# Twelve weight loads moved from GpSimd's queue to SyncE's queue, each in two halves

## The chip, the core and the metric

The kernel runs on one core of one Trainium2 chip. The time is device microseconds of one execution of the whole program; a figure for a kernel is the median of several executions. The profile is one more execution, taken by the hardware profiler. Its rows name the engines PE (TensorE matmul), PEld (TensorE weight load), DVE (VectorE), ACT (ScalarE), POOL (GpSimd) and SP (SyncE). SP computes nothing here: it only issues DMA transfers, in the order of its program. POOL issues DMA transfers too, from a queue of its own.

## The reference

One layer of a decoder trunk on 512 tokens of width 1024, all in float32:

```
h   = RMSNorm(x)
q_a,k_a,v_a, q_b,k_b,v_b, gates = split(h @ W_in)
y_a = block-sparse causal attention with rotary q, k
y_b = stick-breaking causal attention
x   = x + (sigmoid(gate_a)*(y_a @ W_a) + sigmoid(gate_b)*(y_b @ W_b)) @ W_out
h   = RMSNorm(x)
u   = causal_depthwise_conv(h @ W_up, width 3)       # W_up: 1024 x 5632
x   = x + (silu(u_gate) * u_val) @ W_down            # W_down: 2816 x 1024
out = RMSNorm(x)
```

The part that matters here is `h @ W_up`, the up-projection. Its 5632 columns are handled as 22 pairs of column tiles of 128, a gate tile and a value tile in each pair.

## The kernel before

**Three products for one.** A float32 product is made of three TensorE passes: both operands are split into a high part (`hi`, a rounded copy, made by ACT) and a low part (`lo`, what the rounding left, made by DVE), and `mm3` adds hi*hi (line 75), hi*lo (line 76) and lo*hi (line 77). In the up-projection the first operand of each pass is the weight, so line 77 is the pass that reads the low part of the weight, `wlo`; lines 75 and 76 read `whi`.

**Seven products for eight.** Tile pairs 4 to 15 (`MIXED`) use a Strassen-like scheme: seven quarter products (256 columns of tokens each, 12 matmuls each) in place of eight. Their weights are four tiles, called a, b, c and d below with the pair's number behind:

- a: the raw gate tile, and b: a mix of tiles, both loaded by `first_four`;
- c: another mix of tiles, and d: half a raw value tile, both loaded by `last_three`.

a, b and c feed 24 matmuls each, d feeds 12. The mixes were summed in DRAM earlier, as `usum`. For the c tiles the low part was also made earlier, in the attention's merge (`split_ahead`), and written to DRAM as `ulo`. So for c only the high part is made on the spot, and `wlo` is loaded from `ulo` (512 KB); for a, b and d, DVE makes `wlo` (line 900).

**Order of the tiles.** TensorE's order is written out by hand: a4 b4, a5 b5, c4 d4, a6 b6, c5 d5, and so on in rounds of b, c and d of one pair after the a of another, to a15 b15, c14 d14, c15 d15. The last round differs: c15 comes right behind d14, with no a and b between. After d15 come the plain pairs 16 to 21, whose tiles are loaded by `wload` (line 65). The order of all other engines, SP and POOL among them, is set by a scheduler from the code.

**Buffers.** `wmix` takes three tiles per weight: `raw` from a pool of five, `whi` and `wlo` from pools of three. A tile's `wlo` is thus the buffer that the weight three places earlier used. For c of pair i that is d of pair i-1 (for c15 it is b15, for c4 it is b4), so the load of `ulo` into it can start only when TensorE has done the last matmul of that weight. Between the two, TensorE works on a and b of another pair, 48 matmuls; for c15 it works on c14 and d14, 36 matmuls. Of a c tile, half h=1 (columns 512 to 1023) is used first, by the first `quarter` call of `last_three`, and half h=0 by the second, 12 matmuls later.

**Queues.** All loads of `raw` are issued by SP (lines 895 and 65), five buffers ahead. The loads of `ulo` into `wlo` are issued by POOL (line 897), which has nothing else to do in this stage.

Of the kernel before, what the change touches and what calls it, by code (L numbers as in the profile page):

```python
# [10 lines left out]
F32 = mybir.dt.float32  # L11
# [30 lines left out]
def trunk_layer(ctx: ExitStack, tc: tile.TileContext, x: bass.AP, xT: bass.AP, w: bass.AP, vec: bass.AP,  # L42
                gfin: bass.AP, trig: bass.AP, out: bass.AP):
    nc = tc.nc
# [845 lines left out]
    def wmix(i, parts, n=1024, lo=None):  # L890
        raw = wraw.tile([128, 1024], F32, name="raw")
        hi = wsp.tile([128, 1024], F32R, name="whi")
        wlo = wsp.tile([128, 1024], F32R, name="wlo")
        for sl, src in parts:
            nc.sync.dma_start(raw[:, sl] if isinstance(sl, slice) else raw.rearrange("p (h c) -> p h c", h=2), src)
        if lo is not None:
            nc.gpsimd.dma_start(wlo.rearrange("p (h c) -> p h c", h=2), lo)
        nc.scalar.activation(hi[:, :n], raw[:, :n], AF.Copy)  # L898
        if lo is None:
            nc.vector.tensor_sub(wlo[:, :n], raw[:, :n], hi[:, :n].bitcast(F32))  # L900
        return hi, wlo

    def first_four(i):
        wa = wmix(i, [(slice(0, 1024), w[WIDX["up", i, 0]])])
        wb = wmix(i, [(None, both(usum[i][0:2]))])
        ps1, ps2 = up_ps(), up_ps()
        X, Q, Y, Z = ps1[:, :256], ps1[:, 256:], ps2[:, :256], ps2[:, 256:]
        quarter(X, wa, 0, rows_of(0, 0), True)
        quarter(Q, wa, 1, rows_of(1, 0), False)
        quarter(Y, wb, 1, mixed_rows(1), True)  # L910
        quarter(Z, wb, 0, mixed_rows(3), False)
        p1s, p5s, v = (tmp[i % 2][:, n] for n in range(3))
        nc.scalar.activation(p1s, X, AF.Copy)
        nc.scalar.activation(p5s, Y, AF.Copy)
        nc.vector.tensor_add(v, Z, p5s)
        return ps1, ps2, p1s, v

    def last_three(i, ps1, ps2, p1s, v):
        X, Q, Y, Z = ps1[:, :256], ps1[:, 256:], ps2[:, :256], ps2[:, 256:]
        wc = wmix(i, [(None, both(usum[i][2:4]))], lo=ulo.get(i))  # L920
        wd = wmix(i, [(slice(0, 512), w[WIDX["up", i, 1]][:, 512:])], 512)
        quarter(X, wc, 1, mixed_rows(2), False)
        quarter(Y, wc, 0, rows_of(1, 1), False)
        quarter(Z, wd, 0, mixed_rows(4), False)
        u2 = tmp[2][:, i % 2]
        nc.scalar.activation(u2, X, AF.Copy)
        u = up.tile([128, 2, S], F32, name="u", bufs=1)
        nc.vector.tensor_add(u[:, 0, :256], Q, p1s)
        nc.vector.tensor_add(u[:, 1, 256:], X, v)
        nc.vector.tensor_add(u.rearrange("p b s -> p (b s)")[:, 256:768].rearrange("p (n c) -> p n c", n=2),  # L930
                             ps2.rearrange("p (n c) -> p n c", n=2), u2[:, None].to_broadcast([128, 2, 256]))
        glu(i, (u[:, 0], u[:, 1]))
# [228 lines left out]
```

## Time and profile before

| | |
|---|---|
| median of 3 runs | 723.58 us |
| the three runs | 718.51, 723.58, 724.37 us |
| profiled execution, its own time | 722.6 us |
| its span, first to last instruction | 720.6 us |
| PE busy in the span | 705.9 us (98%) |
| DVE, ACT, POOL busy | 568.7, 392.5, 81.8 us |
| mean granted TensorE clock | 0.999 |
| stage of pairs 4 to 15 | about 416.9 to 543.4 us of the span |

The stage limits are the starts of the first and the end of the last matmul on a weight of pairs 4 to 15. In a row of the timeline the columns are the start, the duration (both us), the engine, the line, the operation, and output<-inputs; brackets give the idle time of the engine before the instruction and what ended it. A matmul's duration there includes its way through the array, so that matmuls overlap: the step from one start to the next is the time that TensorE needs for one.

### The profile page before, as it was taken

What the parts mean: (1) busy time and instruction counts of PE and PEld (TensorE: products, weight loads), DVE (VectorE), ACT (ScalarE), POOL (GpSimd) and SP (SyncE); (2) the same over time, 40 slices, a digit from 0 to 9 for tenths busy, and PEclk for the clock granted to TensorE, in tenths of its full rate; (3) what the DMA queues carried; (4) which work ended last, traced back from release to release, by engine and by line L of the source; (5) the groups of instructions that cost most, each with busy time, mean ns of one, the idle gap of its engine ahead of it and who ended that gap; (6) DMA issues with size and microseconds to landing.
All of it is one profiled execution on the core that took longest, in us unless ns stands there. A gap on an engine that the chain in (4) does not pass through costs nothing.

```text
span 720.6 us, 11212 instructions
## 1 busy us (share of the span) xinstructions
PE 705.9 (98%) x4316; PEld 611.2 (85%) x4316; DVE 568.7 (79%) x862; ACT 392.5 (54%) x585; POOL 81.8 (11%) x131
## 2 busy tenths in 40 slices
PE   9999999999999999999999999999989999999996
PEld 6888888879878888888899899999988888888884
DVE  7778867595994685749685998898898778878997
ACT  6335535463654444427485667667665445456764
POOL 1211222354002122000004100000000000000000
PEclk9999999999999999999999999999999999999999
DMA  8799999999325786537668657766773323567703
GB/s 314 273 345 366 355 234 242 239 240 254 98 88 187 257 265 230 199 114 257 227 219 239 157 167 249 239 202 227 245 251 111 109 88 93 178 196 228 272 27 118
DMA packets 45974, 151.32 MB, mean 210 GB/s; under 512 B 5216, under 2 KB 5984, under 8 KB 41824
## 3 DMA queue, kind: packets, MB, share of 16 engines
q1 hardware_dynamic: 33536, 93.64, 38.0%
q0 software_dynamic: 12096, 56.63, 28.5%
q8 instruction: 34, 0.56, 0.3%
q10 hardware_dynamic: 288, 0.33, 0.1%
q14 instruction: 20, 0.16, 0.1%
HBM read 135.90 MB, written 44.04 MB: 250 GB/s over the span
## 4 chain that ended last, share of the span: by engine, by line
PE 88%; DVE 5%; DMA 3%; issue 3%; ACT 2%; POOLq 0%; DVEq 0%; ACTq 0%
PE b L77 11%; PE b L76 11%; PE b L75 11%; PE mm L75 10%; PE mm L77 9%; PE mm L76 9%; PE c L75 4%; PE c L77 4%; PE c L76 4%; PE q L194 3%; DMA wlo<-ulo 3%; PE tp L468 3%; PE tp L446 2%; DVE R L417 1%; PE sc L370 1%
## 5 line engine op out<-in xcount | busy, mean ns | idle before, releaser
L76 PE MATMUL b<-h,whi 128*128 128x256 f32 (+1 forms) x336 | 109.1, 325 | 0.0
L75 PE MATMUL b<-h,whi 128*128 128x256 f32 (+1 forms) x336 | 108.9, 324 | 0.0
L77 PE MATMUL b<-h,wlo 128*128 128x256 f32 (+1 forms) x336 | 108.8, 324 | 0.0
L70 ACT ACTIVATE whi<-raw 128x1024 fp32r<-128x1024 f32 (+2 forms) x70 | 68.6, 986 | 72.9 <-PE b L76 28.3
L71 DVE TENSOR_TENSOR wlo<-raw,whi 128x1024 fp32r<-128x1024 f32 (+2 forms) x70 | 78.5, 1129 | 24.4 <-ACT whi L70 24.1
L75 PE MATMUL mm<-xg,whi 128*128 128x512 f32 x224 | 89.9, 402 | 0.0
L77 PE MATMUL mm<-xg,wlo 128*128 128x512 f32 x224 | 87.5, 391 | 0.0
L76 PE MATMUL mm<-xg,whi 128*128 128x512 f32 x224 | 87.5, 390 | 0.0
L76 PEld LDWEIGHTS b<-h,whi 128*128 128x128 f32 x336 | 64.0, 191 | 5.1 <-DVE h L750 0.2
L77 PEld LDWEIGHTS b<-h,wlo 128*128 128x128 f32 x336 | 64.0, 191 | 5.0
L75 PEld LDWEIGHTS b<-h,whi 128*128 128x128 f32 x336 | 64.0, 191 | 5.0
L620 ACT ACTIVATE whi<-raw 128x1024 fp32r<-128x1024 f32 x45 | 47.0, 1052 | 35.6 <-DVE raw L638 16.1
L898 ACT ACTIVATE whi<-raw 128x1024 fp32r<-128x1024 f32 (+1 forms) x48 | 45.6, 951 | 35.0 <-PE b L76 29.4
L620 DVE TENSOR_TENSOR wlo<-raw,whi 128x1024 fp32r<-128x1024 f32 x45 | 54.6, 1222 | 7.2 <-ACT whi L620 7.2
L77 PE MATMUL b<-xa,wlo 128*128 128x256 f32 x192 | 54.7, 285 | 4.7 <-DMA wlo<-ulo 4.7
L75 PE MATMUL b<-xa,whi 128*128 128x256 f32 x192 | 54.4, 283 | 0.0
L76 PE MATMUL b<-xa,whi 128*128 128x256 f32 x192 | 54.4, 283 | 0.0
L75 PEld LDWEIGHTS mm<-xg,whi 128*128 128x128 f32 x224 | 42.1, 188 | 9.8 <-issue 1.8
L77 PEld LDWEIGHTS mm<-xg,wlo 128*128 128x128 f32 x224 | 42.1, 188 | 9.1
L76 PEld LDWEIGHTS mm<-xg,whi 128*128 128x128 f32 x224 | 42.2, 188 | 7.8
L900 DVE TENSOR_TENSOR wlo<-raw,whi 128x1024 fp32r<-128x1024 f32 (+1 forms) x36 | 37.6, 1045 | 11.1 <-ACT whi L898 10.7
L77 PEld LDWEIGHTS b<-xa,wlo 128*128 128x128 f32 x192 | 36.9, 192 | 5.3 <-DMA wlo<-ulo 5.3
(267 smaller groups left out, 1649.1 us busy)
## 6 DMA issues: line engine op xcount, KB each, us to landing
raw<-w SPq DMA_DIRECT2D x113, 512.0 KB, 4.4
usum<-w POOLq DMA_DIRECT2D x12, 1024.0 KB, 26.2
raw<-usum SPq DMA_DIRECT2D x24, 512.0 KB, 4.5
usum<-w POOLq DMA_DIRECT2D x12, 512.0 KB, 20.7
usum<-usum POOLq DMA_DIRECT2D x24, 256.0 KB, 11.8
praw<-usum POOLq DMA_DIRECT2D x12, 512.0 KB, 4.9
ulo<-praw POOLq DMA_DIRECT2D x12, 512.0 KB, 3.3
wlo<-ulo POOLq DMA_DIRECT2D x12, 512.0 KB, 4.0
```

Source lines behind the costliest of these rows:

```text
L70: nc.scalar.activation(hi[:, sl], raw[:, sl], AF.Copy)
L71: nc.vector.tensor_sub(lo[:, sl], raw[:, sl], hi[:, sl].bitcast(F32))
L75: nc.tensor.matmul(ps, a[0], b[0], start=start, stop=False, **kw)
L76: nc.tensor.matmul(ps, a[0], b[1], start=False, stop=False, **kw)
L77: nc.tensor.matmul(ps, a[1], b[0], start=False, stop=stop, **kw)
L194: nc.tensor.matmul(qk0[c], w0[i][:, (k % 2) * 512 + c * 128:(k % 2) * 512 + (c + 1) * 128], xg[k][:, j], start=(k == 0 and n == 0), stop=( ...
L370: nc.tensor.matmul(scs[h // 2][:, h % 2, o:o + n], Q[i][r0:r0 + 32, c, qt * 128:(qt + 1) * 128], K[i][r0:r0 + 32, d, :n], start=False, sto ...
L446: nc.tensor.transpose(tp[:, h, c:c + 128], a[:, h, c:c + 128], ident)
L468: nc.tensor.matmul(av[h * 64:(h + 1) * 64, j, qt * 128:(qt + 1) * 128], v[:, kb, (2 * p + h) * 64:(2 * p + h + 1) * 64], aT[p][:, h, o + k ...
L620: splits.append((nc.scalar.activation(hi, raw, AF.Copy), nc.vector.tensor_sub(lo, raw, hi.bitcast(F32))))
L898: nc.scalar.activation(hi[:, :n], raw[:, :n], AF.Copy)
L900: nc.vector.tensor_sub(wlo[:, :n], raw[:, :n], hi[:, :n].bitcast(F32))
```

## The change

The load of a c tile's low part is no longer one transfer of 512 KB issued by POOL. It is two transfers of 256 KB issued by SP, half h=1 first. The bits moved are the same; the views as float32 on both sides only make the two types equal.

```
         if lo is not None:
-            nc.gpsimd.dma_start(wlo.rearrange("p (h c) -> p h c", h=2), lo)
+            for h in (1, 0):
+                nc.sync.dma_start(wlo[:, h * 512:(h + 1) * 512].bitcast(F32), lo[:, h].bitcast(F32))
         nc.scalar.activation(hi[:, :n], raw[:, :n], AF.Copy)
```

The order of instructions on PE, DVE and ACT is the same as before. POOL loses its last twelve transfers; SP gains 24. On SP, in the middle of the stage, these rows stand one behind the other in the changed program (+ marks what is new; usum_417, usum_418 and usum_419 are the mixes of pairs 10, 11 and 12, ulo_2583 and ulo_2584 the low parts of c9 and c10, `w 128x512` is a d tile, `w 128x1024` an a tile):

```order
+L898 DMA wlo<-ulo_2583 128x512 x2
 L895 DMA raw<-usum_417 128x2x512
 L895 DMA raw<-w 128x512
 L895 DMA raw<-w 128x1024
+L898 DMA wlo<-ulo_2584 128x512 x2
 L895 DMA raw<-usum_419 128x2x512
 L895 DMA raw<-usum_418 128x2x512
```

The two halves of c10 now stand ahead of the raw loads of b12 and c11 in SP's queue, and the first of them waits there for TensorE to finish d9. In most other rounds the halves stand one place later, behind the raw load of the b tile.

At the end of the stage SP's queue reads as follows (usum_422 is the mix of pair 15, here c15; ulo_2588 and ulo_2589 are the low parts of c14 and c15; the line-65 rows are the tiles of pairs 16 to 21):

```order
 L895 DMA raw<-usum_422 128x2x512
+L898 DMA wlo<-ulo_2588 128x512 x2
 L895 DMA raw<-w 128x512
-L65 DMA raw<-w 128x1024 x12
+L65 DMA raw<-w 128x1024 x3
+L898 DMA wlo<-ulo_2589 128x512 x2
+L65 DMA raw<-w 128x1024 x9
```

The two halves of c15 stand behind the first three loads of the plain pairs and ahead of the other nine.

## The prediction

> **What bounds the kernel now.** I read the page first, then TensorE's waits, then the timeline around each wait.
>
> ```profile
> span 720.6 us, 11212 instructions
> PE 705.9 (98%) x4316; PEld 611.2 (85%) x4316; DVE 568.7 (79%) x862; ACT 392.5 (54%) x585; POOL 81.8 (11%) x131
> ...
> PE 88%; DVE 5%; DMA 3%; issue 3%; ACT 2%; POOLq 0%; DVEq 0%; ACTq 0%
> ...
> L77 PE MATMUL b<-xa,wlo 128*128 128x256 f32 x192 | 54.7, 285 | 4.7 <-DMA wlo<-ulo 4.7
> ```
>
> TensorE is busy for 98% of the span and carries 88% of the chain that ends last. The last line shows where a load costs it time: line 77, the pass that reads the low part of the weight, idles 4.7 us behind the very transfer that the change moves. By stage, with PE busy as the first figure behind the length:
>
> ```profile
> 416.90:545.00 128.10, 123.44 (x1017) 122.52 (x1016) 112.80 (x174) 86.96 (x128) 6.40 (x12) 1.00 0.68 223
> 545.00:701.00 156.00, 156.00 (x689) 129.03 (x688) 133.52 (x166) 83.86 (x107) 0.00 (x0) 1.00 0.46 149
> ```
>
> In the 156 us behind the stage TensorE has no idle time at all, so what the stage gives up should reach the end. In the stage 4.66 us are idle; TensorE's list of waits has one row there:
>
> ```profile
> PE b L77 <- DMA wlo<-ulo: 4.7, 3, 2.7
> ```
>
> Three waits, the longest 2.7 us. In TensorE's timeline:
>
> ```profile
> 488.90 0.28 PE L75 MATMUL b<-xa,whi 128*128 128x256 f32 x1
> 489.02 0.28 PE L76 MATMUL b<-xa,whi 128*128 128x256 f32 x1
> 490.17 0.39 PE L77 MATMUL b<-xa,wlo 128*128 128x256 f32 x1 [0.87 <-DMA wlo<-ulo]
> ...
> 510.31 0.28 PE L76 MATMUL b<-xa,whi 128*128 128x256 f32 x1
> 511.67 0.39 PE L77 MATMUL b<-xa,wlo 128*128 128x256 f32 x1 [1.08 <-DMA wlo<-ulo]
> ...
> 536.12 0.28 PE L76 MATMUL b<-xa,whi 128*128 128x256 f32 x1
> 539.11 0.38 PE L77 MATMUL b<-xa,wlo 128*128 128x256 f32 x1 [2.71 <-DMA wlo<-ulo]
> ```
>
> The undisturbed step is 0.12 us (488.90 to 489.02). The three disturbed ones are 1.15, 1.36 and 2.99 us, so they cost 1.03 + 1.24 + 2.87 = 5.14 us. I take this and not the idle 4.66, since a matmul drawn 0.28 us long covers part of the gap.
>
> The loads behind them, on POOL, and how long each took to land (the last line of the tile view: of all twelve, then of these three alone):
>
> ```profile
> L897 POOL DMA_DIRECT2D wlo<-ulo x12: 528/528/557, 423.2 to 532.2; - x12
> ...
> DMA to landing us min/median/max: 3.5/4.0/6.8
> ...
> 483.67 0.54 POOL L897 DMA_DIRECT2D wlo<-ulo  x1 [9.50 <-DVE u L928]
> DMA to landing us min/median/max: 6.5/6.5/6.5
> 505.00 0.53 POOL L897 DMA_DIRECT2D wlo<-ulo  x1 [9.55 <-DVE tm L857]
> DMA to landing us min/median/max: 6.6/6.6/6.6
> 532.25 0.53 POOL L897 DMA_DIRECT2D wlo<-ulo  x1 [5.23 <-PE b L77]
> DMA to landing us min/median/max: 6.8/6.8/6.8
> ```
>
> They are c10, c12 and c15. Each landed right ahead of the disturbed matmul (483.67 + 6.5 = 490.2). Issue takes half a microsecond every time; what varies is the landing. When the buffer came free:
>
> ```profile
> 483.03 0.28 PE L77 MATMUL b<-xa,wlo 128*128 128x256 f32 x1
> ...
> 531.56 0.28 PE L77 MATMUL b<-xa,wlo 128*128 128x256 f32 x1
> ```
>
> The first is the last matmul on d9, the second on b15. For c10 the buffer is free at 483.31, POOL issues 0.36 us later, and the first use is due at 489.14: 5.83 us in all. A load that lands in 4.0 us is in time; one of 6.5 us is not. c15 is free at 531.84 and due at 536.24, so it has 4.40 us; issued 0.41 us later, its load is just in time at the median of 4.0 us, and late at anything over it.
>
> **The change, part by part.**
>
> *POOL loses twelve issues.* It does nothing else in this stage (6.40 us busy in the row above, twelve issues), and no engine waits for it otherwise: nothing gained beyond the waits.
>
> *SP gains 24 issues, and with the first of each pair a wait on TensorE.* One issue costs what SP's row shows, 0.38 us, thus 0.76 us in a round of some 10 us that now has four:
>
> ```profile
> 482.74 0.38 SPq L895 DMA_DIRECT2D raw<-usum  x1
> DMA to landing us min/median/max: 3.5/3.5/3.5
> ...
> ACT whi L898 <- PE b L76: 29.4, 34, 2.0
> ...
> 492.99 1.06 ACT L898 ACTIVATE whi<-raw 128x1024 fp32r<-128x1024 f32 x1 [0.94 <-PE b L76]
> 494.43 1.06 ACT L898 ACTIVATE whi<-raw 128x1024 fp32r<-128x1024 f32 x1 [0.38 <-PE b L76]
> ```
>
> (The second line is that load's time to land.) Queued behind the wait are the raw loads of c, d, a and b that follow, in c10's round b12 first, then c11. Who waits for them is ACT's split, line 898, and the line of ACT's waits says that these splits wait for a buffer that TensorE frees (34 times); no wait of theirs on a load is listed. b12's load was issued at 482.74 and landed at 486.2; its split ran at 492.99, so it lay ready for 6.7 us. Behind the two halves it is issued at about 483.31 + 0.76 = 484.1, 1.3 us later. c11's split ran at 494.43; its load is next behind b12 and had landed by 490.8:
>
> ```profile
> 484.31 0.38 SPq L895 DMA_DIRECT2D raw<-usum  x1
> DMA to landing us min/median/max: 6.5/6.5/6.5
> ```
>
> That is 3.6 us in hand in one of the slowest rounds, less up to 0.4 us of later issue and 1.0 us because TensorE no longer waits at c10. The cover is still 2 us. Cost: nothing; were the cover gone, it would be the lateness itself, once a round.
>
> *The halves share a queue with the raw loads.* The raw load issued at 484.31 landed at 490.8, 0.7 us behind POOL's c10 load of 483.67, and both took 6.5 us; the raw load of 482.74, with no POOL load beside it yet, took 3.5 us. I read this as two queues taking turns at the same transfer engines. In one queue what is issued later should stay behind. The bound from below is thus the 3.5 us of a load alone; from above, the 6.5 us of a load that shares. No trace here shows a half's landing in this place; the nearest rows of the size are
>
> ```profile
> raw<-w SPq DMA_DIRECT2D x22, 256.0 KB, 4.9
> ...
> raw<-osum SPq DMA_DIRECT2D x4, 256.0 KB, 3.1
> ```
>
> 3.1 to 4.9 us. In c10's round the halves stand ahead of b12's load, so I take 3.5 us for the first half: at about 487, 2 us ahead of 489.14. The second is due 12 matmuls, 1.44 us, after the first. c12 has the same 48 matmuls, 5.8 us, and one raw load ahead of it: even issued in the same moment, 3.5 us and 0.8 us for the half behind it (its rate is below) leave 1.5 us. Both waits go: -1.03 - 1.24.
>
> [...]
>
> *c15, the tight one.* It stands behind three loads of 512 KB for the plain pairs:
>
> ```profile
> 527.09 0.35 SPq L65 DMA_DIRECT2D raw<-w  x1
> DMA to landing us min/median/max: 5.5/5.5/5.5
> 528.24 0.33 SPq L65 DMA_DIRECT2D raw<-w  x1
> DMA to landing us min/median/max: 5.9/5.9/5.9
> 530.26 0.33 SPq L65 DMA_DIRECT2D raw<-w  x1
> DMA to landing us min/median/max: 5.2/5.2/5.2
> ...
> 529.00:539.00 10.00, 7.40 (x62) 7.19 (x60) 9.21 (x17) 7.87 (x13) 0.53 (x1) 1.00 0.97 326
> ```
>
> They landed at 532.6, 534.1 and 535.5, in order. The engines moved 326 GB/s in that stretch (last figure), which puts 0.80 us on a 256 KB half. Behind the third load the first half lands at 535.5 + 0.8 = 536.3, against 536.24; the second at 537.1, against 537.68. So the wait shrinks from 2.87 us to something between 0 and 2.87; I take 0.3 us, near the worked landing. The nine loads behind it are for products after the first three plain tiles.
>
> *Sum.* 5.14 - 0.3 = 4.84 us less. Against the profiled execution's own 722.6 us: 717.8 us. That execution lies 1.0 us under the median of 723.58; since the three runs spread over 5.9 us, more than the waits of the profiled one, part of that spread is probably these waits, and I don't add the 1.0 us.
>
> **The rivals.**
>
> *c15's wait stays whole.* The halves stand behind 1.5 MB of up-loads, and should these land 2.9 us later, as the low-part load ahead of them (c14) now goes through the same queue, only 2.27 us go: 722.6 - 2.27 = 720.3. For it: no slack at all by the sum above. Against it: the same bytes used the same engines before.
>
> *The transfers are late whoever issues them.* The engines ran at 0.97 of their time in that stretch. If the load is slow because the engines are full, another queue saves only the 0.36 to 0.41 us from free buffer to POOL's issue, 1.1 us over the three waits: 721.5. Against it: order in the queue puts later loads behind. [...]
>
> *Slower: SP's queue stalls behind its new wait.* SP holds the raw loads until TensorE is done with d, and each c or b load then comes too late for ACT's split, so TensorE waits for `whi` in every round. It ends slower by over 1% once the new wait exceeds (7.2 + 5.1)/12 = 1.03 us a round: 722.6 - 5.14 + 12 x 1.03 = 729.8. It starts only beyond the 2 us of cover above. Against it: that cover, and 3.6 us where a round is not slow.
>
> *Faster by over 1%.* The fastest run, 718.51, is 4.1 us under the profiled one. If it still held c15's 2.87 us, it would come to 715.6 without. Nothing in the profile shows that it did.
>
> **How the numbers follow.** The forecast (both short waits gone, c15's nearly) has 0.64, c15 whole 0.14, late transfers 0.08, slower 0.04, faster than 1% 0.10. One per cent, about what a measurement of this kernel tells from no change, is 7.2 us: below 716.3 counts as faster. The forecast gives 717.5 to 718.8 (0 to 1.3 us left at c15), the first two rivals 720.3 and 721.5, all within 1%; with tails, faster 0.11, same 0.84, slower 0.05. The range reaches down to 715.6 and up to 721.3, the second case plus the 1.0 us by which the median lies over the profiled execution; it leaves out the late transfers and the slower case.
>
> **What would show it.** Right: no row of TensorE waiting for `wlo<-ulo`; the halves, on SP, landing within about 4 us; the stage from a4 to d15 some 5 us shorter; splits at line 899 still waiting for TensorE. Wrong: a wait of line 77 left at c15 (first rival) or at c10 and c12 with landings of 6 us (second); ACT's splits or line 75 waiting on a load of raw (third). It would also be wrong if the stage shrank and the time did not.

## The result and the profile after

The changed kernel takes 717.41 us (median of 13 executions, 716.99 to 718.94), the kernel before 723.58 us (718.51 to 726.71). The ratio is 0.9928, 95% interval 0.9906 to 0.995: faster, by 0.7%, clear of no change and within the one per cent that the prediction counts as the same. Three executions among all that follow took 1003.76, 2376 and 4027 us (the first of the kernel with the transfer on ScalarE's queue, the others of the kernel before) and are left out of every median and range. The profiled execution's own time is 717.56 us, its span 715.8 us, 4.8 us under that of before.

The page of the changed kernel, with the same lines as shown of before:

```profile
span 715.8 us, 11210 instructions
PE 705.0 (98%) x4316; PEld 610.5 (85%) x4316; DVE 568.1 (79%) x862; ACT 392.0 (55%) x585; POOL 74.8 (10%) x119
...
PE 91%; DVE 5%; ACT 1%; DMA 1%; issue 1%; ACTq 0%
...
L77 PE MATMUL b<-xa,wlo 128*128 128x256 f32 x192 | 54.4, 284 | 0.5 <-DMA wlo<-ulo 0.5
```

And the one row that TensorE's list of waits still has on the transfer:

```profile
PE b L77 <- DMA wlo<-ulo: 0.5, 1, 0.5
```

Of three waits one is left, 0.5 us idle where 4.7 were. It is c15's, in TensorE's timeline:

```profile
533.50 0.28 PE L76 MATMUL b<-xa,whi 128*128 128x256 f32 x1
534.24 0.39 PE L77 MATMUL b<-xa,wlo 128*128 128x256 f32 x1 [0.46 <-DMA wlo<-ulo]
```

A step of 0.74 us in place of 2.99: 0.62 us lost. SP's loads and their landing, that is the time from the issue until all data is there, in the tile view (first all 24 halves; then the first halves of c10, c12 and c15, each asked for alone):

```profile
L898 SPq DMA_DIRECT2D wlo<-ulo x24: 320/374/430, 422.7 to 529.6; - x24
DMA to landing us min/median/max: 2.6/3.8/5.2
...
DMA to landing us min/median/max: 2.6/2.6/2.6
DMA to landing us min/median/max: 3.8/3.8/3.8
DMA to landing us min/median/max: 4.9/4.9/4.9
```

Issued by POOL the three whole transfers took 6.5, 6.6 and 6.8 us. What stood behind them in SP's queue did not become late: the raw load behind c10's halves still lands slowly, 5.9 us (its row in SP's timeline, and its landing):

```profile
484.07 0.38 SPq L895 DMA_DIRECT2D raw<-usum  x1
DMA to landing us min/median/max: 5.9/5.9/5.9
```

The splits still wait for TensorE, as often as before, and not for a load, in ACT's list of waits:

```profile
ACT whi L899 <- PE b L76: 29.0, 34, 2.0
```

The stages by window (a4 to d15, then the 156 us behind it):

```profile
416.90:540.00 123.10, 122.64 (x1016) 122.18 (x1015) 111.53 (x171) 86.32 (x128) 0.00 (x0) 1.00 0.69 232
540.00:696.00 156.00, 156.00 (x689) 128.89 (x689) 134.22 (x168) 83.94 (x108) 0.00 (x0) 1.00 0.45 149
```

TensorE idles 0.46 us in the stage, 4.66 before, and is gap-free behind it as before, so that all of it reaches the end.

### The profile page after: what moved, and what is told of

It reads as the page before. It is cut to its first block, busy times and chain, and to the rows that moved or that the text cites. A ratio compares the mean times of both kernels' runs of the same rounds, so it can differ in the third digit from the quotient of the medians.

```text
span 715.8 us, 11210 instructions
## 1 busy us (share of the span) xinstructions
PE 705.0 (98%) x4316; PEld 610.5 (85%) x4316; DVE 568.1 (79%) x862; ACT 392.0 (55%) x585; POOL 74.8 (10%) x119
## 4 chain that ended last, share of the span: by engine, by line
PE 91%; DVE 5%; ACT 1%; DMA 1%; issue 1%; ACTq 0%
PE b L76 12%; PE b L77 12%; PE b L75 12%; PE mm L75 10%; PE mm L77 10%; PE mm L76 10%; PE c L75 4%; PE c L77 4%; PE c L76 4%; PE q L194 3%; PE tp L468 3%; PE tp L446 2%; DVE R L417 1%; PE sc L370 1%; PE sc L380 1%
```

## The experiments

Medians of the executions are given; the kernel before, run beside each group on the same chip, had medians of 722.0, 722.0, 721.7 and 721.6 us. In the code, + and - mark what differs from the changed kernel or from the kernel before; lines that only follow from it are left out.

**Which part of the edit helps: queue, halves, or their order.** First the whole transfer on SP:

```
-            for h in (1, 0):
-                nc.sync.dma_start(wlo[:, h * 512:(h + 1) * 512].bitcast(F32), lo[:, h].bitcast(F32))
+            nc.sync.dma_start(wlo.rearrange("p (h c) -> p h c", h=2).bitcast(F32), lo.bitcast(F32))
```

> SyncE's queue, but the low part of c in one transfer of 512 KB. Theory 1 (the place in one queue is what helps: loads issued later stay behind): the whole lands when the second half lands in the changed kernel, so c10 at about 487.3 and c12 at 508.5 are in time (due 489.0 and 509.1), and only c15 is later, at 534.9 against 533.6 due: a wait of about 1.3 us in place of 0.62, so 718.1 us. Theory 2 (the halving helps, the transfers are as slow from any queue): c10, c12 and c15 wait as before, about 5 us in all, 721.5 us or more.

717.50 us (716.88 to 718.37), ratio 0.9939 [0.9921, 0.9958]. As the changed kernel: on SP's queue the move alone brings the gain, and the halving nothing that shows. Theory 2's 721.5 us is wrong for this kernel. The wait of 1.3 us that I expected at c15 was 0.4 us idle in the profile: the load landed at 534.42, ahead of the 534.9 at which the changed kernel's second half did.

Second, the same halves on POOL:

```
-                nc.sync.dma_start(wlo[:, h * 512:(h + 1) * 512].bitcast(F32), lo[:, h].bitcast(F32))
+                nc.gpsimd.dma_start(wlo[:, h * 512:(h + 1) * 512].bitcast(F32), lo[:, h].bitcast(F32))
```

> GpSimd's queue as before, but in two halves, first-used half in front. Theory 1: each half still shares the transfer engines with the raw loads issued beside it; the first half of c10 and c12 lands some 5 us after its issue (5.5 us are there), that of c15 about 5.5 us (4.0 are there): waits of 1.5 to 2.5 us in all, 718.8 to 719.5 us, and the executions spread over several us as before. Theory 2: as the changed kernel, 717.4 us.

718.10 us (717.30 to 719.91), ratio 0.9963 [0.9941, 0.9985]. A miss for both theories, 0.7 us from either: without any change of queue, halves bring 3.9 us in the median, where the whole transfer on SP brings 4.5. The first halves of c10, c12 and c15 landed 5.1, 4.7 and 4.1 us after their issue, just inside their slack, and one short wait was left, a step of 0.33 us at c4's second half.

Third, SP's halves in the other order:

```
-            for h in (1, 0):
+            for h in (0, 1):
```

> SyncE's queue, two halves, but the half that is used second is issued first. Theory 1: the first-used half stands behind 256 KB more, lands where the second half landed (0.66 us later at c15) and only c15 feels it: a wait of about 1.3 us, 718.1 us. If the order of the halves does not matter, because both land together: 717.4 us.

718.50 us (717.54 to 718.63), ratio 0.9948 [0.9927, 0.997]: 1.1 us over the changed kernel. The profile has a wait at c15 that explains a part of it (TensorE's waits):

```profile
PE b L77 <- DMA wlo<-ulo: 0.9, 1, 0.9
```

The first use is gated by the second transfer, which landed at 534.60, and the matmul started at 534.65. The step is 1.20 us, so 1.08 us are lost, 0.5 us more than in the changed kernel's profile; the rest of the 1.1 us isn't accounted for. By the medians, halves in the wrong order are 1.0 us worse than no halves, though the two ranges overlap.

**A queue of its own (the "row" of the expectation), or GpSimd's way of issuing?** The whole transfer on ScalarE's queue, which like POOL's is not the one that carries the raw loads:

```
-            nc.gpsimd.dma_start(wlo.rearrange("p (h c) -> p h c", h=2), lo)
+            nc.scalar.dma_start(wlo.rearrange("p (h c) -> p h c", h=2).bitcast(F32), lo.bitcast(F32))
```

> The whole 512 KB issued by ScalarE's queue: a hardware queue like SyncE's, but a row of its own like GpSimd's. Theory 1 (a row of its own takes turns with SyncE's raw loads): landings of 6 to 7 us at c10, c12 and c15 as before and waits of 4 to 5 us in all, 721.5 to 722.5 us. Theory 3 (GpSimd's software queue itself is slow): as SyncE's queue with the whole transfer, 718.1 us. ScalarE's own work may be held up by the wait for TensorE in its queue; by the instruction order it waits there for TensorE anyway, so at most some tenths of a us.

718.14 us (717.36 to 719.69), ratio 0.9946 [0.9926, 0.9967]. Theory 1's 721.5 is wrong. c10 and c12 are in time, but c15 still waits:

```profile
PE b L77 <- DMA wlo<-ulo: 1.4, 1, 1.4
```

The landings of c10, c12 and c15 by ACT:

```profile
DMA to landing us min/median/max: 4.8/4.8/4.8
DMA to landing us min/median/max: 5.6/5.6/5.6
DMA to landing us min/median/max: 5.9/5.9/5.9
```

And of the kernel with the whole transfer on SP:

```profile
DMA to landing us min/median/max: 3.4/3.4/3.4
DMA to landing us min/median/max: 5.1/5.1/5.1
DMA to landing us min/median/max: 4.9/4.9/4.9
```

With POOL's 6.5, 6.6 and 6.8 us, the same 512 KB cost 0.5 to 1.4 us more from a queue of its own than in SP's, and 0.9 to 1.7 us more yet if POOL issues them. Theory 1 and theory 3 seem to hold a part each. But these are single executions, and POOL's own landings differ between profiled executions with this transfer on POOL: 5.9 to 6.9 us at c10, 5.3 to 6.6 at c12, 4.0 to 6.9 at c15. At c12 and c15 that overlaps with ACT's, so the share of each isn't settled. (The view as float32, which only the whole transfers on POOL lack, is no cause that shows: by the profile a whole load is 144 packets and 0.52 MB from POOL without the view and from ScalarE with it.)

**Is POOL's queue too slow as such?** Halves on POOL, with a buffer of 2 KB a partition of its own for the first-used half of every c but c14, so that it is free 2.9 us earlier (24 matmuls of 0.12 us), and far earlier for c15 (the lines that let the matmuls read the two buffers are left out):

```
+            half = clo.tile([128, 512], F32R, name="clo") if i != MIXED[-2] else wlo[:, 512:]
+            nc.gpsimd.dma_start(half.bitcast(F32), lo[:, 1].bitcast(F32))
+            nc.gpsimd.dma_start(wlo[:, :512].bitcast(F32), lo[:, 0].bitcast(F32))
```

> GpSimd's queue, two halves, and the first-used half of each c but c14 has a buffer of its own, free 2.9 us earlier (c15's far earlier). If what matters is the 5.8 us (4.4 at c15) from free buffer to first use, and no queue is too slow as such, TensorE never waits and the time is 717.2 us with a spread of 1 to 2 us, though GpSimd's landings stay at 3 to 6 us. If GpSimd's queue delays the kernel in some other way, it stays at 718.1 us, as with two halves on GpSimd without the buffer.

717.23 us (716.69 to 717.86), ratio 0.9925 [0.9894, 0.9957], and no row of TensorE waiting on the transfer. With halves, then, POOL's queue cost nothing here, with a slack longer than the 5.8 us, or 4.4 at c15, of the kernel before. The earlier buffer without the halves was not run.

**What is left at c15.** The changed kernel, with the first-used half of c15 alone in a buffer of its own (the edit as above, but on SP), and the changed kernel beside it:

```
+            half = clo.tile([128, 512], F32R, name="clo") if i == MIXED[-1] else wlo[:, 512:]
+            nc.sync.dma_start(half.bitcast(F32), lo[:, 1].bitcast(F32))
+            nc.sync.dma_start(wlo[:, :512].bitcast(F32), lo[:, 0].bitcast(F32))
```

> The changed kernel, but the first-used half of c15 has a buffer of its own (2 KB a partition) and is loaded long ahead. If the 0.62 us left at c15 come from its late place behind three up-loads, they go: no wait of TensorE on the low part, 716.8 us. Rival: something else is late next there (the second half, the split of the high part), and the time stays at 717.4 us.

> The changed kernel itself, beside the others on the same chip: 717.4 us, one wait of about 0.5 us idle at c15, executions within 2 us of each other; the kernel before again spreads over 5 us or more.

717.20 us (716.82 to 717.77) against 717.47 us (716.96 to 718.66). The first has no wait left, but the second's profiled execution lost only 0.16 us at c15 too. The difference of 0.27 us has the expected sign, is less than half of the 0.6 us expected and smaller than the spread: it is not shown that this version beats the changed one.

**Where the spread of the kernel before comes from.** Two more profiled executions of it:

> The kernel before, another profiled execution. If the spread of its executions (718.5 to 726.7 us) is that of its waits on the low parts, its time is 717.4 us plus the waits that its trace shows, within about 0.7 us, whatever the waits are; the late loads need not be the same ones.

> The same as the look before, once more: 717.4 us plus the waits on the low parts that its trace shows, within about 0.7 us.

The first took 719.08 us and lost 0.45 us at c10 and 0.84 at c12, nothing at c15: 719.08 - 1.29 = 717.8, as expected. The second took 723.63 us and lost 0.48 at c10, 0.86 at c12, 0.51 at c14 and 2.17 at c15: 723.63 - 4.02 = 719.6, 2.2 us too much. Its timeline shows the rest. After the wait at c15 TensorE starts at the step of 0.12 us, and then, with no wait at all, slows to 0.21:

```profile
538.78 0.39 PE L77 MATMUL b<-xa,wlo 128*128 128x256 f32 x1 [2.01 <-DMA wlo<-ulo]
539.00 0.28 PE L75 MATMUL b<-xa,whi 128*128 128x256 f32 x1
539.12 0.28 PE L76 MATMUL b<-xa,whi 128*128 128x256 f32 x1
...
539.87 0.41 PE L75 MATMUL b<-xa,whi 128*128 128x256 f32 x1
540.08 0.41 PE L76 MATMUL b<-xa,whi 128*128 128x256 f32 x1
```

In windows over the same stretch (the granted clock is the third figure from the end):

```profile
538.00:540.00 2.00, 1.22 (x8) 1.23 (x9) 2.00 (x3) 1.86 (x3) 0.00 (x0) 0.88 0.70 231
540.00:542.00 2.00, 2.00 (x11) 2.00 (x10) 1.89 (x3) 0.38 (x1) 0.00 (x0) 0.50 0.63 244
542.00:543.00 1.00, 1.00 (x6) 1.00 (x6) 0.00 (x0) 0.00 (x0) 0.00 (x0) 0.54 0.02 8
```

The granted clock is halved: of full speed 0.12 x 2 + 0.50 x 2 + 0.46 = 1.7 us are lost, at half speed thus 3.4 us long. That is some 16 steps of 0.21 us in place of 0.12: 1.4 to 1.5 us. With it, 719.6 comes to 718.1, the bound of what I allowed. Every execution has its mean granted clock, so this can be asked of all. To tell whether c15's wait causes it, I left c15 alone on POOL, and then all but c15 (the same with `i == MIXED[-1]` in the condition); what doesn't go by POOL goes by SP in halves:

```
+            if i < MIXED[-1]:
...
+            else:
+                nc.gpsimd.dma_start(wlo.rearrange("p (h c) -> p h c", h=2), lo)
```

> Only c15 goes by GpSimd's queue in one transfer as before; the other eleven by SyncE's queue in halves. Theory 4 (the wait at c15 makes the spread of the kernel before: it is 0 to 3 us long by itself, and when it is long the granted clock of TensorE is often halved for 3.4 us behind it, 1.7 us more): 717.4 to 723 us, median near 720, some executions with a mean granted clock of 0.996 or less, no waits at c10 and c12. Rival (the spread is spread over all late loads): within 2 us of each other, median 717.4 plus up to 2.9 us, clocks of 0.997 and more.

> Only c15 goes by SyncE's queue in halves; the other eleven by GpSimd's queue in one transfer as before. Theory 4: the waits at c10 and c12 stay, 0.5 to 1.2 us each and nearly the same every time: median 719 us, executions within 2 us of each other, no clock under 0.997. Rival: the spread of the kernel before stays, up to 723 us, with clocks of 0.996 and less.

| kernel | median us | range us | executions with clock 0.996 or less |
|---|---|---|---|
| c15 alone on POOL | 720.64 | 718.86 to 722.46 | 6 of 12 |
| all but c15 on POOL | 718.99 | 717.23 to 719.91 | 0 of 12 |
| kernel before, beside these two | 721.62 | 718.00 to 726.22 | 10 of 23 |
| changed kernel | 717.41 | 716.99 to 718.94 | 0 of 13 |

In the first the six with the low clock are the six slowest; of the kernel before beside these two, the ten with the low clock are the ten slowest. The profiled execution with c15 alone on POOL, in TensorE's waits and in windows:

```profile
PE b L77 <- DMA wlo<-ulo: 2.7, 1, 2.7
```

```profile
536.00:538.00 2.00, 1.64 (x10) 1.64 (x11) 2.00 (x3) 0.75 (x2) 0.00 (x0) 0.74 0.86 252
538.00:540.00 2.00, 2.00 (x11) 2.00 (x11) 0.82 (x2) 0.38 (x1) 0.00 (x0) 0.50 0.35 143
```

One wait of 2.7 us idle, and the clock is down to 0.50 right behind it. With all but c15 on POOL the profile has one wait, at c10, and none at c12:

```profile
PE b L77 <- DMA wlo<-ulo: 1.3, 1, 1.3
```

So theory 4 held in the main: c10 and c12 together cost the kernel before some 1.6 us (718.99 against 717.41), c15 3.2 in the median (720.64 against 717.41), half of the time with the clock on top. It did not hold that c10 and c12 wait 0.5 to 1.2 us each and nearly the same every time: here c10 lost 1.4 us and c12 nothing, and the executions lie 2.7 us apart, not within 2. The two prices need not add up: beside these two kernels the one before lies 4.2 us over 717.41.

## Why the prediction was right, point by point

**The sum.** Forecast 717.8, measured 717.41. The profile's own account is the same step by step: 5.14 us of waits before, 0.62 after, so 4.52 of the 4.8 us by which the span shrank; TensorE started a4 0.16 us earlier, too, before anything that was changed. Of the signs set for it, the shorter stage and the waits at line 899 came; "no row of TensorE waiting" and "landing within about 4 us" did not quite, since c15 kept a row of 0.5 us and the halves took up to 5.2.

**c10 and c12 go.** Right. The first halves landed at 485.8 and 507.1; I had put c10's at 487.

**c15 shrinks to 0.3 us.** Right in kind: 0.62 us in one profile and 0.16 in another. I placed the half 0.8 us behind the third load for the plain pairs; that load landed 5.9 us after 527.64, at 533.5, and the half 0.7 us later, at 534.2. The places that I compared were those of the profile before, and they moved: that load was issued 2.6 us sooner than before and landed 1.9 us sooner, and the first use fell due 2.6 us sooner (536.24 before, 533.62 now). The sum held because they moved nearly together, which I had not worked out; and 0.3 us was a choice near a worked 0.1.

**SP's wait costs nothing.** Right: the raw load behind c10's halves was issued at 484.07, as forecast (484.1), and no split waited for one. The cover was enough.

**Two queues taking turns at the engines.** For POOL the sharing is shown, by the packets that the profile lists for each queue (q0 is POOL's, q1 SP's); by what turns is not. Before, SP's load of 482.74 had landed by 486.29, so that what SP moved from there to the landing of c10's load, 490.13, was issued after it, and yet SP moved more than POOL:

```profile
q1 hardware_dynamic: 336, 0.67, 59.8%
q0 software_dynamic: 118, 0.42, 39.2%
```

From issue to landing, a quiet round (c8, landed in 3.5 us) and c15 (6.8 us):

```profile
q0 software_dynamic: 144, 0.52, 46.9%
q1 hardware_dynamic: 188, 0.35, 29.0%
...
q1 hardware_dynamic: 481, 1.72, 67.5%
q0 software_dynamic: 144, 0.52, 25.3%
```

The five profiled executions with whole transfers on POOL have 48 such loads. Beside the 33 that landed within 4.3 us SP moved 0.25 to 0.65 MB, in one case 0.90; beside the 15 that took 4.9 us or more, 0.85 to 2.00 MB. A longer load leaves more time to move things beside it, so the figures alone don't prove the direction; the c10 rows do, for that load. In SP's own queue the raw load behind c10's halves still took 5.9 us, but behind the halves, where it delays nothing: they landed at 485.8 and 487.3, it at 490.0. There the step "in one queue what is issued later should stay behind" held, and it helped. What did not follow is that any queue of its own must be as slow: in ScalarE's queue c10 and c12 landed inside their slack, and the time was 718.1 and not 721.5 us. What decides how the turns fall, and what POOL's issuing adds, stays open. The rival "late whoever issues them", at 721.5, is ruled out by both whole-transfer kernels.

**The halves.** I let them carry the first use at c15. They are not needed for it: SP with one whole transfer is as fast, though halves in the wrong order cost 1.1 us.

**The median of before.** I left out the 1.0 us by which it lies over the profiled execution, as part of the same waits. Leaving it out was right, but the waits don't make all of the spread: the halved clock behind c15 has a part in it, and no row of that first profile showed it. How much of the 1.0 us is the clock is not shown. The medians of the first measurement lie 6.2 us apart, more than the 5.1 us of waits in the profile; against the kernel before in the later groups (721.6 to 722.0 us) the gain is 4.2 to 4.6 us.

## What to carry to other kernels

A load that can start only when a buffer comes free has a slack of its own, from there to its first use. Compare that with the slowest landing, place by place; the place that had least here (the last round, where the pattern of the others breaks off: 4.4 us against 5.8) cost most, 3.2 us in the median against 1.6 for c10 and c12 together. If the slack is short, the queue that carries the loads around it was enough here by itself (717.5 us), and a piece that is used first in front nearly so (718.1); an earlier buffer brought the rest of the gain on top of that piece (717.2), and was not tried alone.

An execution-to-execution spread that one kernel has and its variant doesn't is a finding. Put each execution's granted clock beside its time before putting the spread down to noise.

## What was not expected of the hardware

**A wait of 2.7 us was followed by a halved TensorE clock in one execution and not in another.** After an idle gap of 2.0 us at c15, in the second further execution of the kernel before, the granted clock fell to 0.50 for 3.4 us, by the windows above. After one of 2.7 us, with c15 alone on POOL, it did so too: the two windows above and the one behind them lack 0.26 x 2 + 0.50 x 2 + 0.09 x 2 = 1.7 us of full speed, again 3.4 us at half of it.

```profile
540.00:542.00 2.00, 2.00 (x17) 2.00 (x17) 0.19 (x1) 1.06 (x1) 0.00 (x0) 0.91 0.00 0
```

After 2.71 us in the first profile of before, ending at 539.11, it stayed at 1.00:

```profile
538.00:540.00 2.00, 0.89 (x7) 0.89 (x8) 2.00 (x3) 1.49 (x3) 0.00 (x0) 1.00 0.68 213
540.00:542.00 2.00, 2.00 (x19) 2.00 (x18) 1.56 (x3) 0.42 (x2) 0.00 (x0) 1.00 0.60 211
542.00:543.00 1.00, 1.00 (x11) 1.00 (x10) 0.00 (x0) 1.00 (x1) 0.00 (x0) 1.00 0.04 16
```

So the length of the gap alone does not tell these three apart. Behind the shorter gaps of the first profile (0.87 and 1.08 us) and of the changed kernel's (0.46 us) the clock of the stage is 1.00 as well, and the execution with the 1.4 us gap on ScalarE's queue has a mean granted clock of 0.999, where a loss of 1.7 us in its 716.5 would lower the mean by 0.0024. What decides between the two gaps of 2.7 us is not shown, nor how long a gap must be.

**The same bytes landed at different times from different issuers.** In the three slow rounds, 512 KB landed in 6.5 to 6.8 us from GpSimd's queue in the first profile (4.0 to 6.9 over all profiled executions), 4.8 to 5.9 from ScalarE's, and 3.4 to 5.1 from SyncE's, which also carries the loads around it. ScalarE's and SyncE's figures are from one execution each. GpSimd's slow landings went with what SyncE's queue moved beside them, 0.85 to 2.00 MB against 0.25 to 0.90 beside the others, by the packets above. One landing does not fit: c15's 4.0 us in the first of the further executions of the kernel before, beside which SyncE's queue moved 0.90 MB. Why c15 swings by 3 us, and what GpSimd's issuing adds, stays open.
